# Spreading the rotating weight tiles of a two-layer decoder trunk over eight residues of 512 bytes

## The chip, the cores and the metric

The kernel runs on one core of one Trainium2 chip. The metric is device time in microseconds (us) of one execution. The four compute engines are PE (TensorE, with its weight loads shown apart as PEld), ACT (ScalarE), DVE (VectorE) and POOL (GpSimd); SP only issues DMAs here.

## The reference

Two layers over 512 tokens of width 2048, all in float32, each `x = x + W_out(mixer(rmsnorm(x)) * silu(z))`. The first mixer is a sparse attention with a compressed, a selected and a windowed branch, the second a gated linear recurrence; a final norm follows.

```python
def nsa_mixer(h, pos, w_in, ...):
    proj = h @ w_in                       # q, 6 key/value parts, gate logits, z
    ...
    o = g0 * o_cmp + g1 * o_sel + g2 * o_win
    return (o * jax.nn.silu(z)) @ w_out

def hgrn2_mixer(h, lb, w_in, gnorm_w, w_out):
    q, f, i, z = jnp.split(h @ w_in, ...)
    ...
    return (rmsnorm(o) * gnorm_w * jax.nn.silu(z)) @ w_out

for layer in range(2):
    hn = rmsnorm(x, norm_w[layer])
    x = x + (nsa_mixer, hgrn2_mixer)[layer](hn, ...)
return rmsnorm(x, final_norm_w)
```

## The kernel before

Nearly all of the work is large matrix products with weights that are streamed from DRAM. Each float32 operand is split into two parts of the format fp32r: `hi` is the rounded value and `lo` the rest, and a product is three matmuls, hi by hi, lo by hi and hi by lo. The activations are split once a layer into `hhi` and `hlo`. The weights arrive in the tile `raw` (three buffers) and are split by `split` (lines 75 to 79): ACT casts `whi` from `raw` (L77), then DVE subtracts to get `wlo` (L79). `whi` and `wlo` have four buffers each, every one 128 partitions by 512 values, 2,048 bytes a partition; they are allocated at L91, and at L509 for the gate logits. A scheduler fixes the order on each engine when the program is built, and instructions wait for each other on semaphores.

Four families of matmuls use these tiles. A matmul has a stationary operand, which a weight load brings into the array just before, and a moving operand that streams through it.

- `proj` (L110 to L112) has slices of `whi` and `wlo` stationary, 128 columns each, and `hhi`, `hlo`, `hhi` moving, 512 columns. Each k tile takes whi, whi, wlo in turn. `proj_pair` (L129 to L131) is the same over 256 columns at a time.
- `proj_rows` (L156 to L158) has slices of `hhi` and `hlo` stationary and 256 columns of `whi` or `wlo` moving.
- `out_proj` (L176 to L178) has slices of the mixers' split outputs `ohi` and `olo` stationary and 512 columns of `whi` or `wlo` moving; `out_proj_half` (L196 to L198) does it with 256 columns.

Attention (`weights`, L677, and L653 to L673) keeps per row minima `nm` and sums `sm` in small tiles. `lower_bounds` (L732) makes the constants of the second layer, once, at the end of the block of `nsa` that holds the pool `cpool`; in front of the attention, the group's keys are split into `khi` and `klo`.

SBUF tiles lie in the order in which their pools and tags appear, so a tile's address follows from the sizes before it. With slices of 512 bytes, every k slice of one weight tile has the same address modulo 512.

Of the kernel before, what the change touches and what calls it, by code (L numbers as in the profile page):

```python
# [9 lines left out]
F32 = mybir.dt.float32  # L10
F32R = mybir.dt.float32r
# [23 lines left out]
# 500000 ** (-j / 16) in float32  # L35
# [16 lines left out]
class Trunk:  # L52
# [13 lines left out]
    # ---------------------------------------------------------------- helpers  # L66
    def copy(self, out, in_):
        """Spread plain copies over the two engines that read PSUM."""
        self.flip ^= 1
        if self.flip:  # L70
            self.nc.scalar.copy(out, in_)
        else:
            self.nc.vector.tensor_copy(out, in_)

    def split(self, x, hi, lo, on_pool=False):
        """x = hi + lo exactly, both in float32r."""
        self.nc.scalar.copy(hi, x)  # L77
        eng = self.nc.gpsimd if on_pool else self.nc.vector
        eng.tensor_tensor(out=lo, in0=x, in1=hi.bitcast(F32), op=ALU.subtract)  # L79
# [5 lines left out]

    def split_weights(self, raw, tags=("whi", "wlo"), share=False):
        """(hi, lo) of each k of raw [p, k, n]."""
        _, nk, cols = raw.shape
        parts, step = [], 512 // cols
        for k0 in range(0, nk, step):  # L90
            n = min(step, nk - k0)  # L91
            hi, lo = (self.wpool.tile([128, n, cols], F32R, name=t, tag=t, bufs=4) for t in tags)
            self.split(raw[:, k0:k0 + n, :], hi, lo, share and k0)
            parts += [(hi[:, k, :], lo[:, k, :]) for k in range(n)]
        return parts

    def proj_weights(self, w, c0, c):
        """Half of the weights that proj takes."""
        src = w[c * 1024:(c + 1) * 1024, c0:c0 + 128].rearrange("(k p) n -> p k n", p=128)
        return self.load_split(src, [128, 8, 128])  # L100

    def proj(self, w, c0, ahead=None):
        """(h @ w[:, c0:c0+128]) transposed: [feature, t] in PSUM; ahead: the first half of the weights."""
        acc = self.pproj.tile([128, S], F32, name="acc", tag="acc")
        for c in range(2):
            parts = ahead if ahead and c == 0 else self.proj_weights(w, c0, c)
            for k, (hi, lo) in enumerate(parts):
                kt = c * 8 + k
                first, last = kt == 0, kt == KT - 1
                self.nc.tensor.matmul(acc, hi, self.hhi[:, kt, :], start=first, stop=False)  # L110
                self.nc.tensor.matmul(acc, hi, self.hlo[:, kt, :], start=False, stop=False)  # L111
                self.nc.tensor.matmul(acc, lo, self.hhi[:, kt, :], start=False, stop=last)  # L112
        return acc

    def proj_pair(self, w, ca, cb):
        """Two units at once, over the first half of the tokens before the second half."""
# [17 lines left out]
    def proj_rows(self, w, c0, c1):  # L134
        """h @ (w[:, c0:c0+128] and w[:, c1:c1+128]): for two tiles of tokens each, [t, tile, unit, feature] in PSUM."""
# [25 lines left out]
    def out_proj(self, w, h0, og):  # L161
        """x += o[:, heads from h0] @ w[rows of those heads]; og: (hi, lo) pairs [d, t]."""
# [19 lines left out]
    def out_proj_half(self, w, h0, og, tiles, then):  # L182
        """x += o[:, heads from h0] @ w[rows of those heads]; og: (hi, lo) pairs [d, t]."""
# [21 lines left out]
    def transpose4(self, src, dst):  # L205
        """[a, 4*128] -> [128, 4, a]: four 128 x 128 transposes."""
# [5 lines left out]
    def rows_to_cols(self, pool, rows, n, dst):  # L212
        """[n, 128] in DRAM -> [128, n] in SBUF."""
# [9 lines left out]
    # ---------------------------------------------------------------- constants  # L223
# [6 lines left out]
    def _setup(self, tmp):  # L230
# [22 lines left out]
        # p - j  # L253
# [5 lines left out]
        # 0 where s <= t, else NEG; zeros to the left of the diagonal block  # L259
# [3 lines left out]
        # (128 i + p) - (16 n + 31) >= 0 where compressed block n is over at t  # L263
# [17 lines left out]
    def _rope_tables(self, work):  # L281
# [3 lines left out]
        # inv_freq on the partitions: row j of the literals, picked by p mod 16 == j  # L285
# [11 lines left out]
        # -1 on partitions 0..15, +1 on 16..31  # L297
# [4 lines left out]
        # cos on partitions 0..31, sin on 32..63  # L302
# [26 lines left out]
    # ---------------------------------------------------------------- norms  # L329
    def square_sum(self, t, c, on_dve=False):  # L330
        """Sums of squares over column block c of the rows of x tile t."""
# [11 lines left out]
    def rstd_of(self, t):  # L343
        """1 / sqrt(mean(x^2) + eps) of the rows of x tile t: [128, 1]."""
# [7 lines left out]
    def norm(self, layer, t, scale_on_pe=None, pool=None):  # L352
        """Columns of tile t of hhi + hlo = (x * rstd * norm_w) transposed."""
# [25 lines left out]
    def load_final_norm(self, pool, tags):  # L379
        """The last norm's weights on every partition, in four tiles."""  # L380
# [7 lines left out]
    def last_out_proj(self, w, h0, og, out):  # L388
        """The last rows of the output projection, tile by tile, each with its final norm."""
# [26 lines left out]
    def weighted(self, t):  # L416
        """How many column blocks of tile t have the last norm's weights before its scale."""
        return 2 if t == NT - 1 else 3
# [13 lines left out]
    # ---------------------------------------------------------------- NSA  # L432
# [9 lines left out]
    def values(self, w, g):  # L442
        """Selected and window values of group g as [s, s-tile, branch, d], split."""
# [5 lines left out]
    def blocks(self, cpool, w_in, c0, pos, rotate, midway=None):  # L449
        """Both halves of the compressed blocks' inputs: [d, position in the half, group, half block]."""  # L450
# [26 lines left out]
    def compress(self, cpool, blk, w1, w2, copies):  # L477
        """SiLU hidden layer of the compressed blocks, transposed: [h, group, copy, block]."""
# [18 lines left out]
    def gates(self, w_in):  # L497
        """Sigmoid of the gate logits as [t, t-tile, 3 * heads]."""
        nc = self.nc
        n = 3 * N_HEADS  # L500
        # both parts of the weights side by side: the sums over hi on partitions 0..47, over lo on 48..95
        acc = self.pproj.tile([128, S], F32, name="acc", tag="acc")
        for c in range(2):
            raw = self.wpool.tile([128, 8, n], F32, name="raw", tag="raw")
            nc.sync.dma_start(raw, w_in[c * 1024:(c + 1) * 1024, NSA_GL:NSA_Z].rearrange("(k p) n -> p k n", p=128))
            for k0 in (0, 4):
                w = self.wpool.tile([128, 4, 128], F32R, name="whi", tag="whi", bufs=4)
# [19 lines left out]
    def nsa(self):  # L527
# [6 lines left out]
        with tc.tile_pool(name="cmp", bufs=1) as cpool:  # L534
# [15 lines left out]
            # hi, lo, hi on 32 partitions each  # L550
# [5 lines left out]
        with ExitStack() as es:  # L556
# [4 lines left out]
            for g in range(GROUPS):  # L561
                # the group's keys: 32 compressed, then tiles of 128, selected and window in turn
# [13 lines left out]
                for r in range(0, REP, 2):  # L576
# [3 lines left out]
                    # the last pair's first two tiles of tokens come first, for the output projection  # L580
# [29 lines left out]
    def query(self, w_in, h):  # L610
        """The rotated queries of head h, split."""
# [7 lines left out]
    def gate_z(self, w_in, h, ov):  # L619
        """o * SiLU(z) of head h, split for the output projection."""  # L620
# [10 lines left out]
    def out_group(self, w_out, h):  # L631
        """The output projection of the four heads before head h, behind the work of head h."""
# [3 lines left out]
    def attention(self, h, g, q, keys, vals, order):  # L636
        """The gated sum of the three branches of heads h and h + 1, for two tiles of tokens at a time:
        which they are, and [d, head, tile, t] in PSUM."""
        nc, att = self.nc, self.att
        ps = [self.weights(h + r, order[0], q[r], keys) for r in range(2)]  # L640
        for step, i in enumerate(order):
# [8 lines left out]
            # compressed block  # L650
# [3 lines left out]
            # hi, hi, lo against the values' hi, lo, hi  # L654
# [22 lines left out]
    def weights(self, h, i, q, keys):  # L677
        """The weights of the three branches of head h for the tokens of tile i, times their gates."""
# [5 lines left out]
        # keys 0..288 end at the first bank's end, the rest fills the next two  # L684
# [11 lines left out]
        nm = att.tile([128, 3], F32, name="nm", tag="nm", bufs=4)  # L696
        sm = att.tile([128, 3], F32, name="sm", tag="sm", bufs=4)
        wt = att.tile([128, 3], F32, name="wt", tag="wt", bufs=4)
        # the compressed block's weights in a tile of their own, then three times behind the others
# [31 lines left out]
    # ---------------------------------------------------------------- HGRN2  # L731
    def lower_bounds(self, tmp):  # L732
        """Of the only layer: cumsum of the softmax over layers, minus its first row."""
        nc, pool = self.nc, self.consts
        e, r, self.lb, self.oml = (pool.tile([128, N_HEADS], F32, name=n) for n in ("lbe", "lbr", "lb", "oml"))
# [22 lines left out]
    def level_masks(self):  # L758
# [7 lines left out]
        # all ones, and ones in the columns s = 0, 1 mod 4  # L766
# [6 lines left out]
        # for h = 1 .. 16, at the t in the right half of a block of 2h: s in the left half of the block;  # L773
        # for h = 16 only its second quarter, and its first quarter in the mask after
# [13 lines left out]
    def hgrn(self, out):  # L788
        nc, work, tc = self.nc, self.work, self.tc
        w_in, w_out = self.hgrn_w_in[0], self.hgrn_w_out[0]  # L790
        with ExitStack() as es:
# [13 lines left out]
            # the last two heads go side by side  # L805
# [12 lines left out]
    def hgrn_inputs(self, w_in, h):  # L818
        """i of heads h and h + 1: [s, s-tile, head, feature]."""
# [6 lines left out]
    def hgrn_levels(self, w_in, h):  # L826
        """Attention within the chunks, and what the state takes from head h."""
# [18 lines left out]
        def summed(w, parts):  # L846
            """Sums over d of the columns of w, on every partition s (or those of each part's pick)."""
# [12 lines left out]
        def near(hx):  # L860
            """The levels s == t, h = 1 and h = 2, from products by element."""
# [22 lines left out]
        def scale(x, half, hx, tot, out=None):  # L884
            """One half of each block of 2 hx columns of x, times what lies in the block's other half."""
# [11 lines left out]
        def insert(hx, lv, mask, c0=0):  # L897
            """What lv has for the right halves of the blocks of 2 hx, where the mask says so."""
# [22 lines left out]
        # the levels 8 and 16 from one set of keys: the right halves of level 8, those of level 16 for the  # L921
        # keys of the second quarter, and these over the second quarter as well, for the keys of the first
# [37 lines left out]
    def hgrn_inner(self, h, Q, K, tot, attT, I):  # L960
        """The normalized output of head h: [t, t-tile, feature]."""
# [29 lines left out]
    def hgrn_gate(self, w_in, w_out, h, o):  # L991
        """Norm weight and SiLU(z) on head h, split for the output projection."""
# [44 lines left out]
```

## Time and profile before

| what | value |
|---|---|
| median of two runs | 2061.58 us (2061.51 and 2061.65) |
| span of the profiled execution, first to last instruction | 2057.3 us |
| what lies around the span | about 4.3 us, median minus span |
| PE busy | 2027.9 us of the span |
| DVE, ACT, POOL busy | 1244.3, 862.7 and 78.9 us |
| read from DRAM, written | 173.66 and 4.19 MB |

The profile gives the span of one execution and no separate total for it; the runs' total is taken as the span and what lies around it. A matmul's duration in the profile is longer than the distance from its start to the next one's, because matmuls are pipelined, so the pace of PE is read from the starts in the timeline.

### The profile page before, as it was taken

To read this page: it belongs to the slowest core of one execution; us is meant where nothing else is said; L and a number is where in the kernel's file an instruction comes from. 1 tells how busy PE (TensorE), PEld (TensorE's weight loads), DVE (VectorE), ACT (ScalarE), POOL (GpSimd) and SP (SyncE) were. 2 spreads that over 40 slices of the span, in tenths; PEclk is the share of its full clock that TensorE was granted. 3 is DMA by queue.
4 is the path that set the end of the run, shared out by engine and by line. 5 is a ranking of instruction groups with operands and counts; after the bars stand their busy time and mean duration, and the time that the engine had idled before them with its cause. 6 is when DMAs were issued, how large, how long until landed. Compare 5 with 4: busy or idle time off the path is not lost.

```text
span 2057.3 us, 30342 instructions
## 1 busy us (share of the span) xinstructions
PE 2027.9 (99%) x11666; PEld 1759.2 (86%) x11666; DVE 1244.3 (60%) x2928; ACT 862.7 (42%) x1852; POOL 78.9 (4%) x63
## 2 busy tenths in 40 slices
PE   7999999999999999999999999999999999999997
PEld 7789889888988888889998989889898898988885
DVE  7634676565756575756875656456564565645655
ACT  5223554444535363446733343333432334333344
POOL 5000000000000000001300000000000000000004
PEclk9999999999999999999999999999999999999999
DMA  5353222323232322232423222332322322223233
GB/s 169 82 140 104 72 72 63 92 72 86 60 99 66 92 67 88 62 87 88 155 62 92 73 83 73 92 93 72 93 72 82 97 78 83 73 82 102 77 92 109
DMA packets 272674, 179.83 MB, mean 87 GB/s; under 512 B 8192, under 2 KB 254320, under 8 KB 272528
## 3 DMA queue, kind: packets, MB, share of 16 engines
q1 hardware_dynamic: 272528, 177.88, 29.7%
q8 instruction: 92, 1.51, 0.3%
q14 instruction: 54, 0.44, 0.1%
HBM read 173.66 MB, written 4.19 MB: 86 GB/s over the span
## 4 chain that ended last, share of the span: by engine, by line
PE 95%; DVE 3%; ACT 1%; issue 1%; DMA 0%; SPq 0%; DVEq 0%
PE acc L111 17%; PE acc L110 16%; PE acc L112 16%; PE acc L177 5%; PE acc L176 5%; PE acc L178 4%; PE acc L156 4%; PE acc L157 4%; PE acc L158 4%; PE pt L665 2%; PE lv L951 1%; PE lv L936 1%; PE sc L693 1%; PE sc L691 1%; PE ov L673 1%; PE ov L672 1%
## 5 line engine op out<-in xcount | busy, mean ns | idle before, releaser
L77 ACT CAST whi<-raw 128x512 fp32r<-128x512 f32 x612 | 375.3, 618 | 682.0 <-PE acc L111 455.4
L79 DVE TENSOR_TENSOR wlo<-raw,whi 128x512 fp32r<-128x512 f32 x592 | 409.2, 698 | 392.3 <-ACT whi L77 390.9
L110 PE MATMUL acc<-hhi,whi 128*128 128x512 f32 x1472 | 580.3, 394 | 0.0
L111 PE MATMUL acc<-hlo,whi 128*128 128x512 f32 x1472 | 580.3, 394 | 0.0
L112 PE MATMUL acc<-hhi,wlo 128*128 128x512 f32 x1472 | 579.9, 394 | 0.0
L112 PEld LDWEIGHTS acc<-hhi,wlo 128*128 128x128 f32 x1472 | 276.7, 188 | 58.3
L111 PEld LDWEIGHTS acc<-hlo,whi 128*128 128x128 f32 x1472 | 276.7, 188 | 57.0
L110 PEld LDWEIGHTS acc<-hhi,whi 128*128 128x128 f32 x1472 | 276.8, 188 | 56.2
L156 PE MATMUL acc<-whi,hhi 128*128 128x256 f32 x768 | 217.4, 283 | 0.0
L157 PE MATMUL acc<-wlo,hhi 128*128 128x256 f32 x768 | 216.8, 282 | 0.0
L158 PE MATMUL acc<-whi,hlo 128*128 128x256 f32 x768 | 216.1, 281 | 0.0
L176 PE MATMUL acc<-whi,ohi 128*128 128x512 f32 x416 | 161.7, 397 | 4.2 <-DVE x_all L180 4.1
L177 PE MATMUL acc<-wlo,ohi 128*128 128x512 f32 x416 | 164.2, 395 | 0.0
L178 PE MATMUL acc<-whi,olo 128*128 128x512 f32 x416 | 163.5, 393 | 0.0
L157 PEld LDWEIGHTS acc<-wlo,hhi 128*128 128x128 f32 x768 | 144.8, 189 | 1.1
L156 PEld LDWEIGHTS acc<-whi,hhi 128*128 128x128 f32 x768 | 144.6, 188 | 1.1
L158 PEld LDWEIGHTS acc<-whi,hlo 128*128 128x128 f32 x768 | 144.7, 188 | 0.6
L180 DVE TENSOR_TENSOR x_all<-acc,x_all 128x512 f32<-128x512 f32 x112 | 77.1, 688 | 84.2 <-PE acc L178 83.8
L176 PEld LDWEIGHTS acc<-whi,ohi 128*128 128x128 f32 x416 | 78.4, 189 | 21.2 <-DVE x_all L180 5.3
L714 ACT ACTIVATE p<-p,nm 128x512 f32<-128x512 f32 (+3 forms) x128 | 71.3, 558 | 55.9 <-DVE nm L711 55.3
L177 PEld LDWEIGHTS acc<-wlo,ohi 128*128 128x128 f32 x416 | 78.6, 189 | 17.4 <-DVE wlo L79 2.7
L178 PEld LDWEIGHTS acc<-whi,olo 128*128 128x128 f32 x416 | 78.4, 189 | 16.0
(269 smaller groups left out, 2838.9 us busy)
## 6 DMA issues: line engine op xcount, KB each, us to landing
raw<-in_hgrn_w_in_dram SPq DMA_DIRECT2D x128, 512.0 KB, 4.0
raw<-in_nsa_w_in_dram SPq DMA_DIRECT2D x96, 512.0 KB, 3.7
raw<-in_nsa_w_out_dram SPq DMA_DIRECT2D x40, 512.0 KB, 3.8
raw<-in_hgrn_w_out_dram SPq DMA_DIRECT2D x32, 512.0 KB, 3.8
raw<-in_nsa_w_in_dram SPq DMA_DIRECT2D x32, 256.0 KB, 3.3
out_dram<-x_all SPq DMA_DIRECT2D x16, 256.0 KB, 2.9
x_all<-in_x_dram SPq DMA_DIRECT2D x6, 512.0 KB, 8.2
raw<-in_nsa_ck_w_dram SPq DMA_DIRECT2D x4, 512.0 KB, 4.2
```

The source lines that it names most:

```text
L77: self.nc.scalar.copy(hi, x)
L79: eng.tensor_tensor(out=lo, in0=x, in1=hi.bitcast(F32), op=ALU.subtract)
L110: self.nc.tensor.matmul(acc, hi, self.hhi[:, kt, :], start=first, stop=False)
L111: self.nc.tensor.matmul(acc, hi, self.hlo[:, kt, :], start=False, stop=False)
L112: self.nc.tensor.matmul(acc, lo, self.hhi[:, kt, :], start=False, stop=last)
L156: self.nc.tensor.matmul(acc[:, t, :], self.hhi[:, kt, ts], hi, start=first and t == 0, stop=False)
L157: self.nc.tensor.matmul(acc[:, t, :], self.hhi[:, kt, ts], lo, start=False, stop=False)
L158: self.nc.tensor.matmul(acc[:, t, :], self.hlo[:, kt, ts], hi, start=False, stop=last and t == 1)
L176: nc.tensor.matmul(acc, ohi, hi, start=k == n - 1, stop=False)
L177: nc.tensor.matmul(acc, ohi, lo, start=False, stop=False)
L178: nc.tensor.matmul(acc, olo, hi, start=False, stop=k == 0)
L180: nc.vector.tensor_tensor(out=xs, in0=acc, in1=xs, op=ALU.add)
```

## The change

`whi` and `wlo` get 16 values, 64 bytes, of padding per buffer, through a helper that all allocations of them use. Two small changes make room: `nm` and `sm` become parts of one tile `stat`, and two temporaries of `lower_bounds` move from a pool that lives to the end into `cpool`. Comments and docstrings also go, and lines shift by six or seven; this part of the diff is left out.

```diff
+    def weight_part(self, tag, n, cols):
+
+        pad = 16 if tag in ("whi", "wlo") else 0
+        t = self.wpool.tile([128, 512 + pad], F32R, name=tag, tag=tag, bufs=4)
+        return t[:, :n * cols].rearrange("p (k n) -> p k n", n=cols)
+
     def split_weights(self, raw, tags=("whi", "wlo"), share=False):
...
-            hi, lo = (self.wpool.tile([128, n, cols], F32R, name=t, tag=t, bufs=4) for t in tags)
+            hi, lo = (self.weight_part(t, n, cols) for t in tags)
...
-                w = self.wpool.tile([128, 4, 128], F32R, name="whi", tag="whi", bufs=4)
+                w = self.weight_part("whi", 4, 128)
...
-        nm = att.tile([128, 3], F32, name="nm", tag="nm", bufs=4)
-        sm = att.tile([128, 3], F32, name="sm", tag="sm", bufs=4)
+        stat = att.tile([128, 8], F32, name="stat", tag="stat", bufs=4)
+        nm, sm = stat[:, :3], stat[:, 4:7]
...
-        e, r, self.lb, self.oml = (pool.tile([128, N_HEADS], F32, name=n) for n in ("lbe", "lbr", "lb", "oml"))
+        e, r = (tmp.tile([128, N_HEADS], F32, name=n, tag=n) for n in ("lbe", "lbr"))
+        self.lb, self.oml = (pool.tile([128, N_HEADS], F32, name=n) for n in ("lb", "oml"))
```

The addresses of the built programs, modulo 512 bytes:

| tile | before | after |
|---|---|---|
| hhi, hlo | 128 | 128 |
| raw | 64 | 448 |
| whi, four buffers | 64, 64, 64, 64 | 448, 0, 64, 128 |
| wlo, four buffers | 64, 64, 64, 64 | 192, 256, 320, 384 |
| ohi, olo | 64 | 448 |
| keys and queries in attention (khi, qhi) | 0, 256 | 384, 128 |

The order of instructions and the semaphores that they wait for are the same on PE, POOL and SP. On ACT and DVE they differ in one place, about 160 us into the run, where `lower_bounds` stands next to the first group's key split. ACT before, from the cast of the compressed values (`vcmp`) on:

```order
L551 CAST vcmp<-pt 96x512
L77 CAST khi<-kcmp 128x32
L77 CAST khi<-kr 128x4x128
L738 ACT_TABLE_LOAD
L738 ACTIVATE lbe<-lbe 128x16
L77 CAST whi<-raw 128x512 x2
L435 COPY kr<-acc 128x512
```

And after:

```order
L557 CAST vcmp<-pt 96x512
L745 ACT_TABLE_LOAD
L745 ACTIVATE lbe<-lbe 128x16
L77 CAST whi<-raw 128x512
L77 CAST khi<-kcmp 128x32
L77 CAST khi<-kr 128x4x128
L77 CAST whi<-raw 128x512
L441 COPY kr<-acc 128x512
```

The casts of the keys moved behind the table load, the exponential and one weight cast. DVE before, at the same place:

```order
L552 TENSOR_TENSOR vcmp<-pt,vcmp 32x512
L79 TENSOR_TENSOR klo<-kcmp,khi 128x32
L79 TENSOR_TENSOR klo<-kr,khi 128x4x128
L739 RECIPROCAL lbr<-lbe 128x16
L79 TENSOR_TENSOR wlo<-raw,whi 128x512
L740 TENSOR_TENSOR lbe<-lbe,lbr 128x16
L741 TENSOR_TENSOR lb<-lbe 128x16
L742 TENSOR_SCALAR oml<-lb 128x16
L79 TENSOR_TENSOR wlo<-raw,whi 128x512
```

And after:

```order
L558 TENSOR_TENSOR vcmp<-pt,vcmp 32x512
L746 RECIPROCAL lbr<-lbe 128x16
L79 TENSOR_TENSOR wlo<-raw,whi 128x512
L747 TENSOR_TENSOR lbe<-lbe,lbr 128x16
L748 TENSOR_TENSOR lb<-lbe 128x16
L749 TENSOR_SCALAR oml<-lb 128x16
L79 TENSOR_TENSOR klo<-kcmp,khi 128x32
L79 TENSOR_TENSOR klo<-kr,khi 128x4x128
L79 TENSOR_TENSOR wlo<-raw,whi 128x512
```

The two key subtractions moved from ahead of the first weight subtraction to just ahead of the second.

## Rows read from the trace of the kernel before

**Rows 1.** The page's busy times: busy us, share of the span, instructions.

```profile
PE 2027.9 (99%) x11666; PEld 1759.2 (86%) x11666; DVE 1244.3 (60%) x2928; ACT 862.7 (42%) x1852; POOL 78.9 (4%) x63
```

**Rows 2.** The page's 40 slices: the granted TensorE clock in tenths.

```profile
PEclk9999999999999999999999999999999999999999
```

**Rows 3.** The page's chain that ended last, by engine.

```profile
PE 95%; DVE 3%; ACT 1%; issue 1%; DMA 0%; SPq 0%; DVEq 0%
```

**Rows 4.** Groups by line: out<-in, count | busy us, mean ns | idle before.

```profile
L110 PE MATMUL acc<-hhi,whi 128*128 128x512 f32 x1472 | 580.3, 394 | 0.0
...
L156 PE MATMUL acc<-whi,hhi 128*128 128x256 f32 x768 | 217.4, 283 | 0.0
...
L176 PE MATMUL acc<-whi,ohi 128*128 128x512 f32 x416 | 161.7, 397 | 4.2 <-DVE x_all L180 4.1
...
L196 PE MATMUL acc<-whi,ohi 128*128 128x256 f32 x128 | 36.5, 287 | 1.3 <-ACT hhi L77 1.3
```

**Rows 5.** Timeline of PE in `proj`, 700 to 706 us: start, us, what.

```profile
700.42 0.39 PE L110 MATMUL acc<-hhi,whi 128*128 128x512 f32 x1
...
705.91 0.39 PE L110 MATMUL acc<-hhi,whi 128*128 128x512 f32 x1
```

**Rows 6.** Timeline of PE in `out_proj`, 2018 to 2025 us.

```profile
2018.63 0.39 PE L177 MATMUL acc<-wlo,ohi 128*128 128x512 f32 x1
...
2024.98 0.39 PE L178 MATMUL acc<-whi,olo 128*128 128x512 f32 x1
```

**Rows 7.** Timeline of PE in `proj_rows`, 341 to 345 us.

```profile
341.92 0.28 PE L156 MATMUL acc<-whi,hhi 128*128 128x256 f32 x1
...
344.98 0.28 PE L156 MATMUL acc<-whi,hhi 128*128 128x256 f32 x1
```

**Rows 8.** Timeline of PE in `proj_rows`, 167 to 170 us.

```profile
167.18 0.28 PE L156 MATMUL acc<-whi,hhi 128*128 128x256 f32 x1
...
169.89 0.28 PE L158 MATMUL acc<-whi,hlo 128*128 128x256 f32 x1
```

**Rows 9.** Timeline of PE in `out_proj_half`, 1006 to 1009 us.

```profile
1006.55 0.28 PE L196 MATMUL acc<-whi,ohi 128*128 128x256 f32 x1
...
1008.59 0.28 PE L198 MATMUL acc<-whi,olo 128*128 128x256 f32 x1
```

**Rows 10.** Timeline of PE where `out_proj` begins, 430 to 433 us.

```profile
430.56 0.40 PE L176 MATMUL acc<-whi,ohi 128*128 128x512 f32 x1
...
432.42 0.39 PE L178 MATMUL acc<-whi,olo 128*128 128x512 f32 x1
```

**Rows 11.** Groups of DVE by line and shape.

```profile
L79 DVE TENSOR_TENSOR wlo<-raw,whi 128x512 fp32r<-128x512 f32 x592 | 409.2, 698 | 392.3 <-ACT whi L77 390.9
...
L79 DVE TENSOR_TENSOR olo<-oz,ohi 128x512 fp32r<-128x512 f32 x16 | 11.0, 690 | 6.6 <-ACT ohi L77 6.6
```

**Rows 12.** Groups of ACT by line and shape.

```profile
L77 ACT CAST whi<-raw 128x512 fp32r<-128x512 f32 x608 | 373.9, 620 | 673.2 <-PE acc L111 446.6 <-PE acc L178 82.4 <-PE acc L158 64.6
...
L77 ACT CAST ohi<-zs 128x512 fp32r<-128x512 f32 x14 | 8.6, 619 | 21.2 <-PE acc L177 16.3 <-DVE zs L622 4.8
```

**Rows 13.** Timeline around `lower_bounds`, 161 to 166 us.

```profile
161.34 0.22 ACT L77 CAST khi<-kcmp 128x32 fp32r<-128x32 f32 x1
...
162.10 1.28 ACT L738 ACT_TABLE_LOAD   x1
...
163.52 0.60 ACT L77 CAST whi<-raw 128x512 fp32r<-128x512 f32 x1
...
164.68 0.62 ACT L77 CAST whi<-raw 128x512 fp32r<-128x512 f32 x1 [0.56 <-PE acc L111]
164.71 0.28 PE L156 MATMUL acc<-whi,hhi 128*128 128x256 f32 x1
...
165.34 0.69 DVE L79 TENSOR_TENSOR wlo<-raw,whi 128x512 fp32r<-128x512 f32 x1
```

## The prediction

> **What bounds the kernel now.** I read the busy times first: PE is busy 2027.9 us of a span of 2057.3 us, DVE 60% and ACT 42% [rows 1]. The granted clock is at its upper level, 2.4 GHz, in every slice [rows 2], so no time is to be had from the clock. The chain of waits runs through PE for 95% [rows 3]. So only two things can move the total: the pace of the matmuls that follow each other without waiting, and new waits of PE. Faster or slower splits on ACT and DVE alone change nothing, since both idle hundreds of us before the very casts that the change touches [rows 11, 12].
>
> The groups by line tell how many matmuls touch the moved tiles [rows 4]: three lines of 1,472 in `proj`, so 4,416 of 512 columns; 3 x 768 = 2,304 of 256 columns in `proj_rows`; 3 x 416 = 1,248 of 512 columns in `out_proj`; 3 x 128 = 384 of 256 columns in `out_proj_half`. `proj_pair`, with 384 of 256 columns of which half use these tiles, is small, and I leave it out.
>
> Then the pace, from starts in the timeline. A column a tick at 2.4 GHz would be 213.3 ns for 512 columns and 106.7 ns for 256. What the rows show, with the difference d of residues, moving minus stationary, modulo 512:
> - `proj`, d = 64: 24 steps in 705.91 - 700.42 = 5.49 us, 228.8 ns [rows 5].
> - `out_proj`, d = 0, same 512 columns: 28 steps in 6.35 us, 226.8 ns [rows 6].
> - `proj_rows`, d = 448, 256 columns: 27 steps in 3.06 us, 113.3 ns [rows 7], but in another stretch of the same code and the same residues 23 steps in 2.71 us, 117.8 ns [rows 8].
> - `out_proj_half`, d = 0, 256 columns: 17 steps in 2.04 us, 120.0 ns [rows 9].
> - Where `out_proj` has just taken over from another family, its first 8 steps take 1.86 us, 232.5 ns [rows 10], and only later it settles to the 226.8.
>
> So the pace of a matmul varies by a few ns, and differs between address pairs of equal size. It also has two values for one pair, so the addresses are not the whole of it.
>
> **The change part by part.** *DVE and ACT.* Before, the subtraction for wlo has both inputs and its output on residue 64 and takes 698 ns; the one for olo, from an input on residue 256, takes 690 ns [rows 11]. The cast of whi takes 620 ns from residue 64 to 64, that of ohi 619 ns from 256 to 64 [rows 12]. Spreading residues is therefore worth at most some 8 ns on an instruction that is hidden behind PE anyway: 0 us.
>
> *The merged tile `stat` and the freed constants.* They add no wait and no instruction: 0 us.
>
> *The one reordering.* The first weight cast no longer has the key casts ahead of it, so it comes earlier. The second weight subtraction now has the key subtractions just ahead of it. Before, it ran from 165.34 to 166.03 [rows 13]. After, the table load starts where the first key cast stood, at 161.34; ACT is done with the table load (1.28 us), the exponential and the weight cast (together 0.74 us, from 163.38 to 164.12) and the key casts (0.2 and 0.6 us) near 164.2. DVE then still has the two key subtractions (0.2 and 0.7 us) and the small ones before the second weight subtraction, which I put 0.4 us later than before, ending near 166.4. This wlo is the fourth tile of the batch that PE starts at 164.71, at 12 matmuls of 117.8 ns a tile, so PE reaches it after 36 x 0.118 = 4.2 us, at about 168.9. Cover 2.5 us: 0 us. If that cover were gone and the tile were the second, wanted at 166.2, PE would wait 0.2 us. Behind it on DVE stand the rotation of the next keys, which the attention wants several us later.
>
> *The residues.* After the change the stationary whi of `proj` lies at 448, 0, 64, 128 and wlo at 192 to 384, against hhi at 128. A buffer quartet has 12 uses (whi, whi, wlo by four): two with d = 0, two with d = 64, eight with d of 192, 128, 448, 384, 320 or 256, which no row of 512 columns shows. For the unseen ones I take the middle between the two settled values, 227.8 ns, as nothing ranks them. The mean is (2 x 226.8 + 2 x 228.8 + 8 x 227.8) / 12 = 227.8: 4,416 x 1.0 ns = 4.4 us less.
> `out_proj` loses its d = 0 for the same mixture: 1,248 x 1.0 ns = 1.2 us more.
> For 256 columns the rows run from 113.3 to 120.0 ns; I take the middle, 116.7. `proj_rows` has two paces, and I take it at their middle, 115.6: 2,304 x 1.1 = 2.5 us more. `out_proj_half` falls from 120.0: 384 x 3.3 = 1.3 us less.
>
> Sum: -4.4 + 1.2 + 2.5 - 1.3 = -2.0 us on a span of 2057.3, that is 2055.3, and with the 4.3 us around it 2059.6 us, against a median of 2061.6.
>
> *Bounds of this term.* All at the lowest seen: 4,416 x 2.0 = 8.8, 2,304 x 2.3 = 5.3, 384 x 6.7 = 2.6, together 16.7 us less: 2044.9. All at the highest seen, with 512 columns at 232.5 and 256 at 120.0: 4,416 x 3.7 = 16.3, 1,248 x 5.7 = 7.1, 2,304 x 4.4 = 10.1, together 33.5 us more: 2095.
>
> **The rivals.**
> 1. *The addresses don't matter.* The difference between 228.8 and 226.8 then comes from something else in the two loops. For it: two paces at one address pair [rows 7, 8], and DVE and ACT which don't care [rows 11, 12]. Against it: `proj` and `out_proj` have the same columns and the same pattern of three, and differ in pace. Time: 2061.6. The Trainium skill, "SBUF — State Buffer", section "Who interferes with whom", says that PE and ACT never wait on anyone and that PE has two read ports of its own, one for each operand; by that rule this rival is the whole answer. The trace can't confirm it, as its paces differ.
> 2. *The pace never settles.* Place: `proj`, where whi and wlo now have different d within each group of three, and change again every 12 matmuls. The step just after a change of family is 232.5 ns [rows 10]; if each change of d acts so, 512 columns cost 232.5 and 256 columns 120.0. Price: the upper bound, 33.5 us, 2095. It decides for slower than before once the mean step of `proj` is over 228.8 ns by more than the others gain. Against it: the slow steps of [rows 10] follow a change of the whole kind of matmul, not of the address alone.
> 3. *All settle at the lowest seen*, 2044.9: one d, 64, may have been a bad one, and few of the new ones share it.
> 4. *The lowest steps too hold a stall that spreading removes.* Then 512 columns go to 213.3 and 256 to 106.7: 4,416 x 15.5 + 1,248 x 13.5 + 2,304 x 8.9 = 105.8 us less, 1955.8. Against it: 226.8 at d = 0 and 113.3 at d = 448 are the same 6% over the column time, so that part doesn't look like one of addresses. The Trainium skill, "TensorE: Matmul & The Clock Gate", section "Back-to-back issue gap", gives N / 2.4 + 2.5 ns at the full clock, 215.8 ns for 512 columns. No row here is that short.
>
> **How the numbers follow.** Forecast, a mixture that nearly cancels (2050 to 2070): 0.50. Rival 1: 0.20. Rival 2: 0.14. Rival 3: 0.13. Rival 4: 0.03. The likeliest gives 2059.6 us. The range goes from rival 3 to the middle of rival 2, as waits of part of the matmuls are likelier than of all: 2044 to 2078. Two per cent, 41 us, is about what a measurement of this kernel can tell from no change, and only rival 4 (faster) and more than rival 2's whole price (slower) go past it: 0.03 faster, 0.95 within, 0.02 slower.
>
> **What would show it.** Right: starts in `proj` between 226.8 and 230 ns apart and changing from buffer to buffer, `out_proj` a little over 226.8, PE still over 98% busy with no new releaser in front of its lines, DVE and ACT durations within 10 ns of before. Wrong: settled steps in `proj` over 231 ns or under 225, or PE waiting for wlo near 166 us. If `proj` keeps exactly 228.8 at every residue, rival 1 holds.

## The result and the profile after

The changed kernel takes 2077.38 us (median of two runs, 2076.28 and 2078.48) against 2061.58 us: a ratio of 1.0077 with a 95% interval of 1.0048 to 1.0106. That is 15.8 us slower, where 2.0 us faster was forecast. It lies within 2% and inside the range, on the other side of no change.

The busy times, the clock and the chain of the changed kernel answer to [rows 1 to 3].

```profile
span 2074.1 us, 30342 instructions
...
PE 2044.4 (99%) x11666; PEld 1763.9 (85%) x11666; DVE 1245.5 (60%) x2928; ACT 862.9 (42%) x1852; POOL 79.3 (4%) x63
...
PEclk9999999999999999999999999999999999999999
...
PE 95%; DVE 2%; ACT 1%; issue 1%; DMA 1%; SPq 0%; DVEq 0%; ACTq 0%
```

The span grew by 2074.1 - 2057.3 = 16.8 us and PE's busy time by 2044.4 - 2027.9 = 16.5. DVE, ACT and POOL stand where they stood, the slices of the clock are the same, and the chain runs through PE as before. (On a finer scale, half of the 2.4 GHz is granted for 3.4 us in the last `out_proj` of both kernels, behind a wait of PE, with 1.5 us lost before and 1.4 after, and for the last 4 to 5 us of both spans.) So no engine became late and the clock is no part of the change: PE does the same 11,666 matmuls more slowly.

The groups by line (busy us, mean ns of one | idle before it, releaser) answer to [rows 4, 11, 12]; the lines of the changed kernel are six or seven higher from `proj` on.

```profile
L77 ACT CAST whi<-raw 128x512 fp32r<-128x512 f32 x612 | 375.2, 617 | 691.1 <-PE acc L117 459.6
L79 DVE TENSOR_TENSOR wlo<-raw,whi 128x512 fp32r<-128x512 f32 x592 | 409.9, 699 | 398.4 <-ACT whi L77 396.9
L117 PE MATMUL acc<-hlo,whi 128*128 128x512 f32 x1472 | 583.4, 396 | 0.0
L116 PE MATMUL acc<-hhi,whi 128*128 128x512 f32 x1472 | 582.0, 395 | 0.0
...
L162 PE MATMUL acc<-whi,hhi 128*128 128x256 f32 x768 | 219.3, 286 | 0.0
...
L182 PE MATMUL acc<-whi,ohi 128*128 128x512 f32 x416 | 163.0, 400 | 4.2 <-DVE x_all L186 4.2
```

The cast and the subtraction cost at eight residues (617 and 699 ns) what they cost at one (620 and 698), and PE idles in front of none of these lines more than before. A matmul's mean of 396 ns overlaps its neighbours, so the pace has to be read from starts. PE in the timeline of `proj` (start, us, what) shows two paces within one call:

```profile
699.97 0.40 PE L116 MATMUL acc<-hhi,whi 128*128 128x512 f32 x1
...
703.24 0.39 PE L118 MATMUL acc<-hhi,wlo 128*128 128x512 f32 x1
...
706.24 0.39 PE L116 MATMUL acc<-hhi,whi 128*128 128x512 f32 x1
...
708.98 0.39 PE L116 MATMUL acc<-hhi,whi 128*128 128x512 f32 x1
```

The first two rows are 14 steps apart, 3.27 / 14 = 233.6 ns, with whi at residue 0 and then 448; the last two are 12 apart, 2.74 / 12 = 228.3, with whi at 128 and then 64. Before, it was 228.8 throughout [rows 5]. In `out_proj`, where [rows 6] had 226.8:

```profile
1836.67 0.39 PE L182 MATMUL acc<-whi,ohi 128*128 128x512 f32 x1
...
1842.92 0.40 PE L182 MATMUL acc<-whi,ohi 128*128 128x512 f32 x1
```

27 steps in 6.25 us are 231.5 ns. And in `proj_rows`, where [rows 7] had 113.3:

```profile
343.45 0.28 PE L162 MATMUL acc<-whi,hhi 128*128 128x256 f32 x1
...
348.08 0.29 PE L162 MATMUL acc<-whi,hhi 128*128 128x256 f32 x1
```

39 steps in 4.63 us are 118.7 ns.

Where the time went is the sum over all steps by family, each from a matmul's start to the start of PE's next one, of whatever family. The settled pace, here and below, is the mean of the steps without a stall, under 260 ns for 512 columns and under 150 ns for 256; in `proj` of these two kernels no step lies between 242 and 300 ns.

| family | sum before, us | after | change | settled before, ns | after |
|---|---|---|---|---|---|
| `proj` | 1025.0 | 1032.2 | +7.2 | 229.5 | 231.2 |
| `proj_rows` | 278.1 | 283.6 | +5.5 | 115.5 | 117.9 |
| `out_proj` | 294.7 | 299.3 | +4.6 | 228.4 | 232.2 |
| `out_proj_half` | 49.5 | 49.3 | -0.2 | 119.5 | 117.9 |
| `proj_pair` | 50.1 | 49.6 | -0.5 | 117.8 | 115.9 |

Together 16.6 us, which is the whole of PE's 16.5 and, within 0.2 us, of the span's 16.8.

### The profile page after: what moved, and what is told of

Same layout as the page of the kernel before. It is cut to its first block, busy times and chain, and to the rows that moved or that the text cites. A ratio compares the mean times of both kernels' runs of the same rounds, so it can differ in the third digit from the quotient of the medians.

```text
span 2074.1 us, 30342 instructions
## 1 busy us (share of the span) xinstructions
PE 2044.4 (99%) x11666; PEld 1763.9 (85%) x11666; DVE 1245.5 (60%) x2928; ACT 862.9 (42%) x1852; POOL 79.3 (4%) x63
## 4 chain that ended last, share of the span: by engine, by line
PE 95%; DVE 2%; ACT 1%; issue 1%; DMA 1%; SPq 0%; DVEq 0%; ACTq 0%
PE acc L117 17%; PE acc L116 16%; PE acc L118 16%; PE acc L183 5%; PE acc L182 5%; PE acc L184 5%; PE acc L162 4%; PE acc L163 4%; PE acc L164 4%; PE pt L671 2%; PE lv L958 1%; PE sc L697 1%; PE sc L699 1%; PE sc L698 1%; PE lv L943 1%; PE ov L679 1%
## 5 line engine op out<-in xcount | busy, mean ns | idle before, releaser
L720 ACT ACTIVATE p<-p,stat 128x512 f32<-128x512 f32 (+3 forms) x128 | 71.2, 557 | 56.3 <-DVE stat L717 55.7
```

## The experiments

Three theories had to be told apart. *Own price*: each difference of residues, moving minus stationary, has its pace, and the new ones are dear. *Change*: it is the change of residue from tile to tile that slows the matmuls. *Side edits*: the merged `stat`, the freed constants or the reordering. All kernels below stand beside the kernel before on the same chip, where its median was 2059.7 to 2060.8 us.

**One residue for all, nine times.** The padding is taken away, and a filler ahead of the weight pool puts `raw`, `whi`, `wlo`, `ohi` and `olo` on one residue. Every tile behind the filler moves with them; the order of the instructions is the same on every engine in all nine and in the changed kernel.

```diff
-        pad = 16 if tag in ("whi", "wlo") else 0
+        pad = 0 if tag in ("whi", "wlo") else 0
+        self.fill = consts.tile([128, F // 4], F32, name="fill")   # F bytes; none in u448
```

u64 puts the tiles back on the residue of before, so only the side edits are left.

> The changed kernel without the padding, with a filler tile that puts the weight tiles back on residue 64 (difference 64 to hhi): only the side edits are left (the merged tile of minima and sums, the moved temporaries, the one reordering). Theory A (each pair of residues has its own price) and theory B (a change of residue from one matmul or buffer to the next unsettles the pace, any uniform residue settles low) both expect the kernel before: 2061 to 2063 us, proj 228.8 to 229.5 ns a step, out_proj settling at 226.8. Theory C (the side edits cost the 16 us) expects 2075 to 2079 us.

> As u64, but all weight tiles on residue 128, the residue of hhi: difference 0 in proj and proj_rows, uniform. Theory A, from the steps of the changed kernel whose whi lies at 128 (about 230.8 ns in proj, 120 ns in proj_rows): proj +1.5 ns on 4416 steps and proj_rows +4.5 ns on 2304, 2070 to 2082 us. Theory B: proj settles at the 226.8 ns that out_proj shows at difference 0, 2045 to 2058 us. Theory of no address effect at all: 2061 to 2063 us.

> All weight tiles on residue 192, difference 448 in proj, uniform. Theory A, from the changed kernel's steps whose wlo lies at 192 (about 233 ns in proj, 117.8 in proj_rows): +4 ns on 4416 steps and +2 on 2304, 2078 to 2088 us. Theory B: 2050 to 2063 us, proj at 226.8 to 229 ns.

> The changed kernel with no padding and no filler: all weight tiles on residue 448, difference 192 in proj, uniform. Theory A, from the changed kernel's steps whose whi lies at 448 (about 233 ns in proj, 118 in proj_rows): 2078 to 2088 us. Theory B: 2050 to 2063 us, proj at 226.8 to 229 ns. In all four runs out_proj keeps difference 0 and is the control: 226.8 ns once settled.

The four that followed fill in the other multiples of 64.

> All weight tiles on residue 0: difference 128 in proj, 384 in proj_rows; out_proj and out_proj_half stay at difference 0 as controls (228.4 and 119.5 ns mean). Theory A (a price for each difference of residues modulo 512): the changed kernel's steps with whi at 0 give 233 ns in proj and 118.6 in proj_rows, 2080 to 2088 us. Theory A with period 256 instead of 512: no row yet for this pair of classes, it must equal u256. Theory B is out by the last four runs (u192 and u448 are uniform and slow).

> All weight tiles on residue 256: difference 384 in proj, 128 in proj_rows. Theory A with period 512: not known, between 226.7 and 233.2 ns in proj, 2058 to 2085 us. With period 256: the same as u0, within 2 us and 0.3 ns a step.

> All weight tiles on residue 320: difference 320 in proj, 192 in proj_rows. Theory A with period 256: proj as at difference 64 (229.5 ns), proj_rows as at difference 448 (115.5 ns), 2060 us. With period 512: not known, 2058 to 2085 us.

> All weight tiles on residue 384: difference 256 in proj and in proj_rows. Theory A with period 256: as u128, 227.8 ns in proj, 119.6 in proj_rows, 2061 us. With period 512: another value, 229 to 233 ns, 2063 to 2085 us.

A ninth went between them, at a multiple of 32, since it would have been the cheapest edit to beat both kernels.

> Edit: padding 0 and a filler of 160 bytes, so that raw, whi, wlo, ohi and olo all lie on residue 96: the difference is 32 in proj and 224 in proj_rows. Theory bands (the price changes in steps of 64 bytes): proj as at 0, 227.75 ns, proj_rows as at 192, 115.5: about 2052 us. Theory smooth (the price lies between its neighbours): proj 228.6, proj_rows 117.5, about 2057 us. Theory alignment (an address off a multiple of 64 bytes costs by itself): proj over 230 ns, 2067 us or more.

Settled paces in ns, differences modulo 256; the times are of one execution each, u96's the median of four:

| kernel | time, us | `proj`, difference | pace | `proj_rows`, difference | pace |
|---|---|---|---|---|---|
| u128 | 2061.18 | 0 | 227.8 | 0 | 119.6 |
| u384 | 2062.50 | 0 | 227.8 | 0 | 119.6 |
| u64 | 2060.66 | 64 | 229.5 | 192 | 115.6 |
| u320 | 2059.13 | 64 | 229.5 | 192 | 115.6 |
| u0 | 2081.51 | 128 | 232.6 | 128 | 118.8 |
| u256 | 2079.73 | 128 | 232.6 | 128 | 118.8 |
| u192 | 2079.55 | 192 | 233.2 | 64 | 116.7 |
| u448 | 2079.07 | 192 | 233.2 | 64 | 116.9 |
| u96 | 2083.38 | 32 | 233.2 | 224 | 118.3 |

The timeline of `proj` in u128, 36 steps apart:

```profile
699.25 0.39 PE L118 MATMUL acc<-hhi,wlo 128*128 128x512 f32 x1
...
707.41 0.39 PE L118 MATMUL acc<-hhi,wlo 128*128 128x512 f32 x1
```

And in u448, 42 steps apart:

```profile
699.26 0.39 PE L118 MATMUL acc<-hhi,wlo 128*128 128x512 f32 x1
...
709.06 0.39 PE L118 MATMUL acc<-hhi,wlo 128*128 128x512 f32 x1
```

8.16 / 36 = 226.7 ns against 9.80 / 42 = 233.3, in the same code with one filler's difference.

What follows: the side edits cost nothing (u64 has the pace and, within 1 us, the time of before). A single residue without any change can be slow by 19 us (u192, u448), so the change theory isn't needed for a slow kernel. The price belongs to the difference and repeats every 256 bytes: the four pairs of rows in the table agree within some 0.1 ns. It is a difference and not an address, since `out_proj`, whose two operands move together and keep the difference 0, has 228.5 to 228.6 ns in all nine. (`hhi` and `hlo` lie at 128 in every kernel, so the other differences were made by moving the weights alone.) And it isn't smooth: 32 lies between 0 and 64 and costs as much as 192, so of the three guesses for u96 the last came out (1.0111, 1.0098 to 1.0125), with the addition that it is the difference that must not be off: `out_proj` has both operands on residue 96 there and keeps 228.5 ns. For 256 columns the order is another one: 0 is the dearest, 192 the cheapest. That comes with the columns and not with the exchanged operands, as `proj_pair`, which has 256 columns and the weights stationary, has the same order: 119.7 at 0, 117.8 at 64, 118.6 and 118.8 at 128, 114.3 and 115.4 at 192.

The same prices stand in the changed kernel itself. Sorted by the buffer that they read, the settled steps of its `proj` take 229.4 ns at the difference 0, 229.7 at 64, 232.6 at 128 and 233.0 at 192, about a thousand steps each.

**Each family at its own cheap difference.** `proj` wants 0 and `proj_rows` wants 192, from the same tiles. So the tiles are padded by 256 bytes and the families with 256 columns write and read theirs 192 bytes further in. The pads need 2 KB of room, which the shared rotation `tmp` gives for `sw`, the scratch of `rope`. mixcheap is the same without the shift.

```diff
+        pad = 64 if tag in ("whi", "wlo") else 0
+        off = 48 if pad and cols == 256 else 0      # mixcheap: 0
+        return t[:, off:off + n * cols]...
-        sw = self.work.tile([64, S], F32, name="sw", tag="sw", bufs=1)
+        sw = self.work.tile([64, S], F32, name="sw", tag="tmp", bufs=3)
```

> Edit: filler of 192 bytes, whi and wlo padded by 256 bytes (residues 128 and 384, both 0 against hhi modulo 256), and proj_rows and out_proj_half write and read their parts 192 bytes into the tile; sw shares the rotation tmp to make room. Theory A (each difference modulo 256 has its price for the bytes that are read, wherever the tile begins): proj at 0 costs 227.75 ns as in u128, proj_rows at 192 falls from 119.6 to 115.5 ns, 2,304 x 4.1 = 9.4 us less than u128, out_proj_half from 119.5 to about 116, 1.3 us less: about 2050.5 us, ratio 0.9955 against before. Theory B (it is the tile's base, or any change of residue from buffer to buffer, that counts): no better than u128, 2061 us or more.

> Edit: as best, with no shift inside the tile, so whi and wlo alternate between residues 128 and 384 from buffer to buffer. Theory A (period of 256 bytes, a change of residue by itself costs nothing): the same as u128 and u384, proj 227.75 ns, proj_rows 119.6, 2061 to 2062 us. Theory B (a change of residue from buffer to buffer costs): proj over 229 ns, 2067 us or more. If the shared rotation of sw costs, PE's busy time stays and waits come in.

best took 2072.34 us (1.0060, 1.0047 to 1.0074), mixcheap 2080.03. The paces are what the prices ask: `proj` 227.8 in both, though the residue changes by 256 from buffer to buffer; `proj_rows` 119.6 in mixcheap and 115.6 in best. But both have a wait that no kernel above had, the first of PE's largest waits in mixcheap (us in total, times, longest; the second, at the start, has 6.8 us in the kernel before too):

```profile
PE acc L163 <- ACT kr L443: 10.2, 3, 4.1
PE pt L227 <- DMA nwrows<-in_norm_w_dram: 6.7, 1, 6.7
```

`proj_rows` waits for an accumulator, which ACT can't copy out since the tile `kr` of the shared rotation isn't free: the copy starts only when DVE has made `olo` from `zs`, a tile of the same rotation. And each such wait costs more than its length. Two stretches of mixcheap, the first with the longest wait, the second right behind it (start and end, us; busy time of PE, PEld, DVE, ACT and POOL; granted clock; DMA):

```profile
346.00:350.50 4.50, 0.39 (x5) 0.19 (x3) 3.57 (x7) 2.18 (x4) 0.00 (x0) 0.96 0.00 0
350.50:353.00 2.50, 2.50 (x12) 2.50 (x13) 2.29 (x6) 0.29 (x1) 0.00 (x0) 0.50 0.00 0
```

PE idles, and then 0.50 of the clock is granted, the level of 1.2 GHz: a matmul of 256 columns takes 213 ns there, and 41 such steps behind the three waits cost another 3.8 us. The room, not the residues, made best slow.

Two other ways of making room were tried. best2 keeps no `sw`: the accumulator that has just been copied out is the scratch. u128room is u128 with that alone.

```diff
-        nc.vector.stream_shuffle(sw[32:], q[:32], ...)
+        nc.vector.stream_shuffle(acc[32:64], q[:32], ...)      # and acc[:32] for sw[:32]
```

> Edit: as best, but sw keeps no tile at all: the rotation uses the accumulator that it has just been copied out of as its scratch. Theory A (prices by the difference modulo 256): no wait of best is left, proj 227.7 ns, proj_rows 115.5, out_proj_half 116: 2,304 x 4.1 + 384 x 3.5 = 10.8 us less than u128, about 2050.5 us, ratio 0.995 with an interval below 1. Rival: the accumulator is held longer and PE waits for it, or the waits of mixcheap came from the padded tiles: 2060 us or more.

> Edit: u128 with the scratch of the rotation in the accumulator, so the control of best2. If holding the accumulator costs nothing: as u128, 2061 us, ratio 1.000 to 1.001. If it costs: more, with PE waiting for DVE in front of proj or proj_rows.

best2 took 2059.64 us (0.9999, 0.9990 to 1.0008), u128room 2069.40 (1.0039, 1.0027 to 1.0052). best2 is 9.8 us under its control, where 10.8 were expected; the steps of `proj_rows` (119.6 to 116.4 ns) and `out_proj_half` (119.5 to 116.0) make 7.5 of it. But u128room is 8.2 us over u128. In its waits there is now a row that u128 doesn't have:

```profile
PE acc L116 <- DVE kr L446: 2.8, 1, 2.8
```

That is the price of holding the accumulator longer, and here too half the clock follows, for 3.4 us, which lose 1.7 in `proj`. Another 2.7 us go in 13 steps at half the clock in the last `out_proj`, of which the profiled execution of u128 has none; the rest are longer waits in `out_proj`.

best3 goes over the tokens in four pieces with a quarter of the scratch, and lets the softmax's weights overwrite its sums.

```diff
-        sw = self.work.tile([64, S], F32, name="sw", tag="sw", bufs=1)
+        sw = self.work.tile([64, 128], F32, name="sw", tag="sw", bufs=1)
+        for c in range(0, S, 128):       # shuffle, two products and the sum, on 128 tokens each
-        wt = att.tile([128, 3], F32, name="wt", tag="wt", bufs=4)
+        wt = sm
```

> Edit: as best (whi and wlo at difference 0 in proj, proj_rows and out_proj_half reading 192 bytes into the tile), but the rotation keeps a scratch of its own of a quarter of the size and goes over the tokens in four pieces, and the softmax's weights overwrite the sums. Theory A: proj 227.7 ns, proj_rows 115.5 to 116.4, out_proj 228.4, out_proj_half 116, and no new wait of PE, as ACT frees the accumulator as before: 8.8 to 10.8 us less than u128, so 2050.5 to 2052.5 us, ratio 0.995 to 0.996. Rival: the rotation, with 12 more DVE instructions in each of 28 calls, makes PE wait: 2057 us or more.

best3 took 2054.51 us (median of 8, ratio 0.9972, 0.9961 to 0.9982): 5.5 us under the kernel before, which is some 21 us under the changed one (15.8 + 5.5), with as many buffers for the weights. Its busy times:

```profile
span 2053.1 us, 30770 instructions
...
PE 2022.9 (99%) x11666; PEld 1759.7 (86%) x11666; DVE 1287.4 (63%) x3348; ACT 862.4 (42%) x1852; POOL 79.2 (4%) x63
```

DVE works 43 us more than before, hidden, and PE is busy 5.0 us less. The settled paces are the expected ones (`proj` 227.8, `proj_rows` 116.3, `out_proj` 228.4, `out_proj_half` 116.2 ns). That it is 2 us over its expectation stands in `out_proj`, whose steps sum to 296.9 us against 293.5 in u128 at the same settled pace, so in its stalled steps: 1.4 us are the stretch at half the clock, which u128 lacks, and the rest lies in the first layer. There the scheduler fixed another order of the matmuls, as it did over shorter stretches in best and best2, so best3's 5.5 us are those of layout, room and order together. The paces alone would give 4,416 x 1.7 less in `proj`, 384 x 3.3 less in `out_proj_half` and 2,304 x 0.8 more in `proj_rows`, so 6.9 us less. The mean of `proj_rows` is made of two paces. Its timeline early in the program, 27 steps apart, and later, 24 apart:

```profile
169.80 0.28 PE L164 MATMUL acc<-wlo,hhi 128*128 128x256 f32 x1
...
172.98 0.28 PE L164 MATMUL acc<-wlo,hhi 128*128 128x256 f32 x1
...
1252.97 0.28 PE L164 MATMUL acc<-wlo,hhi 128*128 128x256 f32 x1
...
1255.71 0.28 PE L164 MATMUL acc<-wlo,hhi 128*128 128x256 f32 x1
```

3.18 / 27 = 117.8 ns and 2.74 / 24 = 114.2, at one difference, just as in [rows 7, 8]. In u128, at the difference 0, the same stretch has 120.0:

```profile
169.72 0.28 PE L163 MATMUL acc<-wlo,hhi 128*128 128x256 f32 x1
...
172.96 0.28 PE L163 MATMUL acc<-wlo,hhi 128*128 128x256 f32 x1
```

**Does a change cost as well?** If each matmul paid its own price only, `out_proj` in the changed kernel would stand at the mean of the four prices, (227.8 + 229.5 + 232.6 + 233.2) / 4 = 230.8 (taking `proj`'s prices for it), and it stands at 232.2. Four kernels let the difference change in different rhythms. In lo128, lo64 and hi0lo64 it changes within each group of three (whi at 0, wlo elsewhere), in alt128 from one buffer to the next.

```diff
+        pad = 64 if tag in ("whi", "wlo") else 0    # alt128: 32, and no off
+        off = 32 if tag == "wlo" else 0             # lo64: 16; hi0lo64: 16 on whi
```

> Edit: as mixcheap, but wlo is shifted by 128 bytes inside its tile, so that in proj whi has the difference 0 and wlo 128. Theory N (what counts is the moving tile against the weights that are loaded meanwhile for the next matmul): the middle line of proj, which runs while wlo is loaded, goes from 227.7 to about 232 ns, the third line stays at 227.7. Theory O (what counts is the matmul's own weights): the third line goes to 232, the middle one stays. Either way about 1,472 x 4.3 = 6.3 us on proj and 416 x 4.3 = 1.8 us on out_proj more than mixcheap: about 2069 us.

> Edit: whi at difference 0 and wlo at 64 in proj (both cheap when alone: 227.75 and 229.5 ns), scratch in the accumulator. Theory P (each matmul pays the price of its own difference): lines 227.7, 227.7 and 229.5 ns, about 1,472 x 1.8 = 2.6 us more on proj, 2.1 less on proj_rows, 0.7 more on out_proj, 2062 us. Theory S (a change of the difference between neighbouring matmuls costs by itself): the second and third lines of proj at 232 to 233 ns as in lo128, over 13 us more, 2075 us.

> Edit: whi and wlo padded by 128 bytes, so that both have the difference 0 in one buffer and 128 in the next; scratch in the accumulator. Theory P (own price): proj (227.75 + 232) / 2 = 229.9 ns, 9.5 us more; proj_rows 0.9 less, out_proj 2.6 more: about 2072 us. Theory S (the change itself costs, though it comes only every 12 matmuls in proj and every 3 in out_proj): proj stays near 229.9 and out_proj goes to 232 or more, about 2075 us.

> Edit: as best3, but filler of 128 bytes and, for every shape of tile, whi shifted by 64 bytes and wlo not: in proj hhi minus whi is 0 and hhi minus wlo 64, both cheap when alone (227.75 and 229.5 ns). Theory P (each matmul pays for its own difference): proj lines 227.8, 227.8, 229.5, mean 228.3 ns, and 2063 us with proj_rows at about 118.3. Theory S (a change between neighbours costs by itself, 1.5 to 2 ns a matmul as in lo128 and lo64 above their prices' mean): proj mean 229.8 to 230.3 ns, out_proj 230 or more, about 2071 us.

The expectation for lo64 has a sign wrong: with wlo 64 bytes above `hhi`, the difference in `proj` is -64, that is 192, a dear one. Hence hi0lo64, which has the two cheap ones. Settled paces of `proj`, by line and in the mean, with the mean that own prices would give:

| kernel | time, us | wlo's difference | hi by hhi | hi by hlo | lo by hhi | mean | own prices |
|---|---|---|---|---|---|---|---|
| lo128 | 2089.78 | 128 | 228.0 | 232.3 | 233.6 | 231.2 | 229.4 |
| lo64 | 2084.23 | 192 | 229.2 | 229.5 | 234.6 | 231.1 | 229.6 |
| hi0lo64 | 2076.50 | 64 | 230.0 | 230.5 | 232.7 | 231.2 | 228.4 |
| alt128 | 2082.02 | 0 or 128, as whi | 231.9 | 230.2 | 231.0 | 231.0 | 230.2 |

The lines' figures leave out the few matmuls that stand next to another family; alt128's are means over both kinds of buffers. The times can't be compared with each other, as lo128 has the shared rotation and its waits, lo64 and alt128 the scratch in the accumulator, and hi0lo64 the room of best3; the paces can, as mixcheap, u128room and best3, which have the same order of matmuls as these four, all have `proj` at 227.8. PE in `proj` of hi0lo64, 30 steps apart:

```profile
699.70 0.39 PE L118 MATMUL acc<-hlo,whi 128*128 128x512 f32 x1
...
706.65 0.40 PE L118 MATMUL acc<-hlo,whi 128*128 128x512 f32 x1
```

6.95 / 30 = 231.7 ns, though each of its two differences alone costs under 230. So a change does cost: 1.5 to 2.8 ns a matmul above the own prices where it comes within each three, 0.8 where it comes every 12. `out_proj`, where the moving tile changes from matmul to matmul, has 231.8 in alt128 and 232.4 in hi0lo64. The changed kernel shows a form of it. Of the 12 matmuls in `proj` that read one buffer at the difference 0, the first takes 233.0 ns in the mean, the next six 228.7 to 232.2 and the last five 225.9 to 226.8. u128 has this run-in only where `proj` follows another family: 234.1 to 229.0 ns in the first seven steps, 226.6 to 226.7 from the eleventh on. Both theories that lo128 was to tell apart fall as they were put: neither the middle line alone nor the third alone got dear, but both.

In the changed kernel the cost of changes is small, as its whi and wlo of one turn have the same difference modulo 256 (448 and 192, 0 and 256, and so on). By own prices `proj` would take (230.8 - 229.5) x 4,416 = 5.7 us more, `proj_rows` (117.7 - 115.5) x 2,304 = 5.1, and `out_proj` (230.8 - 228.4) x 1,248 = 3.0: 13.8 of the 16.6 us. The other 2.8 are, by this reckoning, the changes and the stalled steps; no run takes them away alone.

## Why the prediction was wrong

- *PE bounds the kernel, the clock gives nothing, and only paces and new waits can move the total*: right. The 16.8 us are PE's steps, and no wait came in. (Around the span lie 2.2 us in the changed kernel's profiled execution, 2076.28 against 2074.1, and 2.1 in later ones of the kernel before, and not the 4.3 of the sum; no difference hangs on it.)
- *Splits on DVE and ACT, the merged `stat`, the freed constants, 0 us*: right. u64, which has nothing but the side edits, is within 1 us of before.
- *The reordering, 0 us*: right. DVE in the changed kernel, and the matmul that first takes this wlo:

```profile
166.00 0.69 DVE L79 TENSOR_TENSOR klo<-kr,khi 128x512 fp32r<-128x512 f32 x1 [0.33 <-ACT khi L77]
166.61 0.68 DVE L79 TENSOR_TENSOR wlo<-raw,whi 128x512 fp32r<-128x512 f32 x1
...
169.72 0.28 PE L163 MATMUL acc<-wlo,hhi 128*128 128x256 f32 x1
```

  The second weight subtraction ends at 167.29 instead of the 166.4 that I put, since the key casts on ACT began only at 165.23, behind DVE's `lb` by the profile. PE was later too, at 169.72 instead of 168.9, so 2.4 us of cover were left where I had 2.5.
- *The residues, -2.0 us in sum*: wrong, and here is the step: "For the unseen ones I take the middle between the two settled values, 227.8 ns, as nothing ranks them." The two seen differences, 0 and 64, are the two cheap ones. The unseen, 128 and 192 modulo 256, cost 232.6 and 233.2 ns, above both. So `proj` stood at 231.2 ns and not at 227.8: 2.5 of the 3.4 ns come from these two differences, and 0.9 from 0 and 64, which stood there at 229.4 and 229.7 and not at the settled 226.8 and 228.8. The 228.8 of before, read from a settled stretch, is 229.5 in the mean. So the term was +7.2 us instead of -4.4, and that of `out_proj`, which gave up the cheapest difference, +4.6 instead of +1.2, with the price of changes in it. A middle between two samples says nothing of what lies outside them, and a row spoke of it: the 232.5 ns of [rows 10]. I used it for the bound only. The sign of being wrong that I had named, steps in `proj` over 231 ns, is there.
- *`proj_rows`, +2.5 us*: the sign and the pace before (115.6) were right; after, it stands at 117.9 and not at the middle of 116.7, +5.5. *`out_proj_half`, -1.3 us*: its pace fell by 1.6 ns and not by 3.3, and its sum by 0.2 us.
- *Rival 1, the addresses don't matter*: falls with u192, 19 us slower than u64 by a filler alone. The rule of the Trainium skill ("SBUF — State Buffer", section "Who interferes with whom") that PE never waits on anyone may hold between engines; the runs show that PE's own two operands are not indifferent to each other's address.
- *Rival 2, the pace never settles*: the right side, at half its price (15.8 of 33.5 us). Its mechanism was the smaller part: u448 has a settled 233.2 ns without any change of difference, while hi0lo64 and the run-in at the difference 0 show that changes cost too. My argument against it, that the slow steps follow a change of the whole kind of matmul, was no argument against dear differences.
- *Rivals 3 and 4*: fall. `proj` and `out_proj` have no mean under 227.8 ns in any run, and the lowest stretch shown, u128's 226.7, is far from 213.3.
- *Range and chances*: 2077.4 lies in 2044 to 2078 by 0.6 us, and that is luck: the upper end was half of rival 2's price, and most of the time came by another mechanism. Within 2% had 0.95.

## What to carry to other kernels

Where PE bounds a kernel with back-to-back matmuls, the byte difference between the moving and the stationary operand is worth a measurement by a filler in front of a pool: here it was 2 to 3.5% of a matmul's pace. Spreading addresses averages cheap and dear differences and adds the price of changes; better is to give each family of matmuls one cheap difference and keep it from one matmul to the next. And room made for such a layout has its own price: of three ways to find 2 KB, one cost more than the gain and one nearly all of it. (best3, the third, is a gain of 0.3%.)

## What the runs showed of the hardware that was not expected

- The settled step of a matmul depends on the difference of its operands' addresses with a period of 256 bytes: 227.8, 229.5, 232.6 and 233.2 ns for 512 columns at 0, 64, 128 and 192, and 233.2 at 32. For 256 columns in `proj_rows` it is 119.6, 116.8, 118.8 and 115.6, and 118.3 at 224.
- A change of the difference from matmul to matmul costs some 3 ns even between two cheap ones (hi0lo64, 231.2 against 228.4); a change by 256 costs nothing (mixcheap, 227.8). At the difference 0 the pace comes down only over some seven matmuls behind a change, from 233 to under 227 ns.
- `proj_rows` at the difference 192 has two paces, 113.3 to 114 and 117.8 ns, that hold for a whole stretch each. What picks one was not found, and what in the memory makes the prices was not tried.
